# Seven-product weights that begin 256 bytes into their tiles instead of 128

## The chip, the cores and the metric

The kernel runs on one core of a Trainium2 chip. The metric is the device time of one execution in microseconds (us), the median of several runs. TensorE (PE in the rows, with PEld for its weight loads) multiplies, VectorE (DVE) and ScalarE (ACT) prepare operands and evacuate results, GpSimd (POOL) and SyncE (SP) mostly issue DMAs.

## What is computed

One layer of a decoder trunk with sequence 512 and model width 1024, in float32: a combined input projection, gated linear attention (GLA), dilated window attention in three head groups, a gated merge, a squared-ReLU MLP of width 4096, and a sigmoid-gated side input, each behind an RMSNorm. Cut to its products:

```
h   = rmsnorm(x) @ w_in                      # 1024 x 9744, split by columns
mix = (sigmoid(gA) * (oA @ w_o_gla) + sigmoid(gB) * (oB @ w_o_attn)) @ w_out
x  += mix
x  += square(relu(rmsnorm(x) @ w_mlp1)) @ w_mlp2
x  += sigmoid(rmsnorm(x) @ w_pg) * (p @ w_pp)
out = rmsnorm(x)
```

## The kernel before

Every float32 operand is split in two numbers of a reduced format (float32r): `hi`, a rounded copy made by ScalarE, and `lo`, the rest, made by VectorE. A product of two such operands is three matmuls on TensorE: hi with hi, hi with lo, lo with hi.

A weight arrives by DMA as a tile `w` of 128 partitions by 1024 numbers. `fetch` runs a few operands ahead: ScalarE writes the `hi` tile (L244), VectorE the `lo` tile (L239). Both tiles come from `split_weights`. There are 251 such operands, in the fixed order of `OPERANDS`.

Some products are done plainly, with matmuls that stream 512 columns. Others (28 groups, `strassen`) are done in two-by-two blocks with seven block products in place of eight. Their weights are seven operands to a group: four blocks and three sums of blocks. One operand, a stage, is 24 matmuls, each with a 128x128 stationary operand and 256 moving columns, recorded in `run` (L258). In most groups the weight is the stationary operand and an activation (a half of a `ur` tile) moves; in five groups (`v0`, `v1`, `v2`, `gv0`, `gv1`, with `tm=True`) the activation is stationary and the weight moves. In the rows, "mmt<-ur,hi" names the moving operand first and the stationary one second. Side work (attention, GLA, the operand sums) is put between pieces of eight matmuls.

The lines that the change and the argument touch:

```
    def split_weights(tag, i, bufs):
        t = wsp.tile([P, 1024 + PAD], F32R, tag=tag, name=tag, bufs=bufs)
        o = SHIFT if OPERANDS[i] not in UNIT or UNITS[UNIT[OPERANDS[i]]][1] in QUADS else 0
        return t[:, o:o + 1024]
...
                    if tm:
                        c, r = slice(n * P, (n + 1) * P), slice(pr * 256, (pr + 1) * 256)
                        three = ((xh[:, c], wh[:, r]), (xl[:, c], wh[:, r]), (xh[:, c], wl[:, r]))
                    else:
                        c = slice((2 * pr + n) * P, (2 * pr + n + 1) * P)
                        three = ((wh[:, c], xh), (wh[:, c], xl), (wl[:, c], xh))
```

Addresses, in bytes within a partition: a split weight tile is 1152 numbers, 4,608 bytes, nine times 512. The raw weight tiles are 4,096 bytes and the activation tiles 2,048. The three pools stand one behind the other, so all these tiles begin at the same remainder modulo 512. The slices that a matmul takes of them begin at multiples of 512 bytes. So for every seven-product matmul the weight's start and the activation's start differ, modulo 512 bytes, by exactly the shift; for all other products of such tiles, by nothing. "Distance" means this difference below.

The GLA part has 120 matmuls of the same kind, float32r with 256 moving columns (`mm3`, L863), whose operands are all unshifted activation tiles: their distance is nothing.

Of the kernel before, what the change touches and what calls it, by code (L numbers as in the profile page):

```python
# [136 lines left out]

NU, NW, PIECE, WAYS = 71, 5, 8, 2

PAD, SHIFT = 128, 32  # L140

NRAW = 6

# [1418 lines left out]
```

## Time and profile before

| | |
|---|---|
| median of 3 runs | 966.31 us (965.92 to 967.74) |
| the profiled execution | 966.74 us, of which the span from first to last instruction is 964.9 us |
| TensorE busy | 99% of the span, granted clock 0.998 |
| weight loads busy | 93% |
| VectorE, ScalarE, GpSimd busy | 77%, 56%, 11% |

The profiled execution is 0.43 us above the median. Busy time of TensorE counts overlapping matmuls once, and each matmul's record reaches over the start of the next two, so the pace is read from starts: the length of a piece of the chain divided by its matmuls.

### The profile page before, as it was taken

The page shows a single profiled execution, that of the slowest core. Times are in us where ns is not written, and L with a number is a line of the kernel's source. Part 1 is how long each engine was busy: PE and PEld are TensorE (multiplying, and loading weights), DVE is VectorE, ACT ScalarE, POOL GpSimd, SP SyncE. Part 2 cuts the span into 40 slices and gives each one's busy share as a digit, 9 for nine tenths or more (in the row PEclk, how much of TensorE's full clock was granted, in tenths as well). Part 3 has the DMA queues.
Part 4 walks back from the last instruction along what each step waited for, and adds up shares of the span by engine and source line. Part 5 has one row for each costly group of instructions (what it writes and reads, how often), then busy time and mean ns, then how long its engine had stood idle before and what let it go on. Part 6 is the DMA issues. An engine that isn't in the chain of part 4 may idle for free.

```text
span 964.9 us, 16746 instructions
## 1 busy us (share of the span) xinstructions
PE 956.2 (99%) x6732; PEld 893.7 (93%) x6732; DVE 745.4 (77%) x1068; ACT 537.4 (56%) x878; POOL 104.0 (11%) x145
## 2 busy tenths in 40 slices
PE   9999999999999999999999999999999999999997
PEld 7789999999998999999988899999998998988886
DVE  7787879676788769978955788777767899787754
ACT  7346546445666677665732446555655674345633
POOL 0140010420001021013001000010000100000000
PEclk9999999999999999999999999999999999999999
DMA  8565555874446646455536437556654474563102
GB/s 294 159 201 128 153 135 129 236 199 135 110 109 186 164 102 157 113 154 182 169 91 205 119 78 185 153 140 168 170 158 109 113 180 103 132 196 108 44 1 88
DMA packets 41470, 138.93 MB, mean 144 GB/s; under 512 B 5363, under 2 KB 6975, under 8 KB 41392
## 3 DMA queue, kind: packets, MB, share of 16 engines
q1 hardware_dynamic: 27936, 93.29, 29.6%
q0 software_dynamic: 12160, 42.20, 22.1%
q10 hardware_dynamic: 1296, 2.36, 0.7%
q8 instruction: 53, 0.87, 0.4%
q14 instruction: 25, 0.20, 0.1%
HBM read 131.50 MB, written 8.17 MB: 145 GB/s over the span
## 4 chain that ended last, share of the span: by engine, by line
PE 97%; DVE 1%; issue 1%; DMA 1%; ACT 0%; SPq 0%; POOLq 0%; POOL 0%; DVEq 0%; ACTq 0%
PE mmt L258 84%; PE smt L258 4%; PE smt L863 1%; PE smt L803 1%; PE smt L728 1%; DMA u<-in_xT_dram 1%; PE mmt L478 1%; PE mmt L479 0%; PE mmt L477 0%; PE smt L701 0%; PE smt L820 0%; PE smt L819 0%; PE smt L809 0%; PE smt L700 0%; PE smt L991 0%
## 5 line engine op out<-in xcount | busy, mean ns | idle before, releaser
L258 PE MATMUL mmt<-ur,hi 128*128 128x256 f32 (+1 forms) x3152 | 645.3, 302 | 0.0
L258 PEld LDWEIGHTS mmt<-ur,hi 128*128 128x128 f32 x3152 | 506.0, 188 | 24.8 <-issue 1.9
L258 PE MATMUL mmt<-ur,lo 128*128 128x256 f32 (+1 forms) x1576 | 476.9, 303 | 0.0
L239 DVE TENSOR_TENSOR lo<-w,hi 128x1024 fp32r<-128x1024 f32 x251 | 304.2, 1218 | 49.5 <-PE mmt L258 32.1
L244 ACT ACTIVATE hi<-w 128x1024 fp32r<-128x1024 f32 x251 | 262.5, 1054 | 93.2 <-PE mmt L258 28.0
L258 PEld LDWEIGHTS mmt<-ur,lo 128*128 128x128 f32 x1576 | 296.8, 188 | 11.9 <-issue 0.4
L258 PE MATMUL mmt<-hi,ur 128*128 128x256 f32 (+3 forms) x736 | 153.7, 305 | 0.0
L357 ACT ACTIVATE ur<-u 128x512 fp32r<-128x512 f32 x132 | 78.5, 624 | 105.3 <-DVE u L1098 30.9
L258 PEld LDWEIGHTS mmt<-hi,ur 128*128 128x128 f32 x736 | 118.5, 189 | 5.6
L350 DVE TENSOR_TENSOR u<-u,mmt 128x512 f32<-128x512 f32 (+1 forms) x124 | 78.3, 657 | 44.8 <-PE mmt L258 44.6
L258 PE MATMUL mmt<-lo,ur 128*128 128x256 f32 (+3 forms) x368 | 112.2, 305 | 0.0
L365 DVE TENSOR_TENSOR ur<-u,ur 128x512 fp32r<-128x512 f32 x131 | 86.2, 684 | 17.6 <-ACT ur L357 16.9
L332 ACT ACTIVATE u<-mmt 128x512 f32<-128x512 f32 x104 | 61.6, 592 | 55.8 <-PE mmt L258 55.5
L258 PEld LDWEIGHTS mmt<-lo,ur 128*128 128x128 f32 x368 | 69.4, 188 | 2.7
L221 POOL DMA_DIRECT2D w<-in_wts_dram x28 | 24.9, 890 | 356.2 <-DVE w L218 258.3
L210 POOL DMA_DIRECT2D w<-in_wts_dram x28 | 25.8, 921 | 276.5 <-DVE ur L365 52.8
L258 PE MATMUL smt<-ur,hi 128*128 128x512 f32 x144 | 44.7, 390 | 0.1
L224 DVE TENSOR_TENSOR w<-w 128x1024 f32<-128x1024 f32 x28 | 34.3, 1225 | 1.0
L218 DVE TENSOR_TENSOR w<-w 128x1024 f32<-128x1024 f32 x28 | 34.3, 1225 | 1.0
L258 PEld LDWEIGHTS smt<-ur,hi 128*128 128x128 f32 x144 | 26.9, 188 | 6.0 <-DVE ur L365 0.5
L258 PE MATMUL smt<-ur,lo 128*128 128x512 f32 x72 | 28.2, 391 | 0.0
L390 ACT ACTIVATE u<-u 128x512 f32<-128x512 f32 x24 | 14.9, 622 | 16.5 <-DVE u L1179 16.5
(210 smaller groups left out, 715.0 us busy)
## 6 DMA issues: line engine op xcount, KB each, us to landing
w<-in_wts_dram SPq DMA_DIRECT2D x167, 512.0 KB, 4.2
w<-in_wts_dram POOLq DMA_DIRECT2D x56, 512.0 KB, 5.8
u<-in_xT_dram SPq DMA_DIRECT2D x8, 256.0 KB, 5.1
v_dram<-u POOLq DMA_DIRECT2D x8, 256.0 KB, 6.2
u<-v_dram POOLq DMA_DIRECT2D x8, 256.0 KB, 6.6
y_dram<-u ACTq DMA_DIRECT2D x8, 256.0 KB, 2.4
u<-y_dram POOLq DMA_DIRECT2D x8, 256.0 KB, 6.0
u<-in_xT_dram POOLq DMA_DIRECT2D x8, 256.0 KB, 8.6
```

The costliest lines, as they stand in the source:

```text
L210: GP.dma_start(w, wts[UNIT[f"{q}.A22"]], accum_op=OP.add)
L218: V.tensor_tensor(w, w, raw[f"{q}.A11"], op=OP.add)
L221: GP.dma_start(w, wts[UNIT[f"{q}.A21"]], accum_op=OP.add)
L224: V.tensor_tensor(w, w, raw[f"{q}.A12"], op=OP.add)
L239: V.tensor_tensor(lo, w, hi.bitcast(F32), op=OP.subtract)
L244: S.activation(hi, w, AF.Copy)
L258: TE.matmul(o, lhsT=l, rhs=r, start=a, stop=b, skip_group_check=shared)
L332: S.activation(sums[c], bank[b], AF.Copy, scale=-scale if c[0] else scale)
L350: V.tensor_tensor(out, s, ps, op=OP.subtract if m else OP.add)
L357: S.activation(hi, x, AF.Copy)
L365: V.tensor_tensor(lo, x, hi.bitcast(F32), op=OP.subtract)
L390: S.activation(t, x, AF.Square, scale=1.0 / 32.0)
```

## The change

`SHIFT` is counted in numbers of four bytes. The padded tile size stays, and so do all tile addresses. Of the 251 split operands, the 196 of the seven-product groups are written, and read by TensorE, 128 bytes further on in their tiles; the other 55 stay at the start. The instructions on every engine, their order and their waits are the same.

```
-PAD, SHIFT = 128, 32
+PAD, SHIFT = 128, 64
```

## Rows read from the trace of the kernel before

**Rows 1.** The page's first part: busy time, share of the span and instructions of each engine.

```profile
PE 956.2 (99%) x6732; PEld 893.7 (93%) x6732; DVE 745.4 (77%) x1068; ACT 537.4 (56%) x878; POOL 104.0 (11%) x145
```

**Rows 2.** The chain that ended last, by engine; then all that TensorE waited for, by line: total us, times, longest us.

```profile
PE 97%; DVE 1%; issue 1%; DMA 1%; ACT 0%; SPq 0%; POOLq 0%; POOL 0%; DVEq 0%; ACTq 0%
...
PE smt L452 <- POOL ones L447: 1.0, 1, 1.0
PE mmt L478 <- DVE ur L367: 0.3, 1, 0.3
PE mmt L477 <- ACT ur L359: 0.3, 1, 0.3
```

**Rows 3.** TensorE's groups by line and shape: the four kinds of seven-product matmul (256 columns), and the GLA kind of L863. Columns: busy us, mean ns of one, idle time before.

```profile
L258 PE MATMUL mmt<-ur,hi 128*128 128x256 f32 x2576 | 467.0, 283 | 0.0
L258 PE MATMUL mmt<-ur,lo 128*128 128x256 f32 x1288 | 364.4, 283 | 0.0
L258 PE MATMUL mmt<-hi,ur 128*128 128x256 f32 x560 | 101.3, 283 | 0.0
L258 PE MATMUL mmt<-lo,ur 128*128 128x256 f32 x280 | 79.3, 283 | 0.0
L863 PE MATMUL smt<-ur 128*128 128x256 f32 x120 | 16.9, 283 | 0.0
```

**Rows 4.** The chain in order of time, four long pieces made of seven-product matmuls alone: start us, length us, what, count.

```profile
95.85 49.37 PE mmt L258 x416
159.96 14.39 PE mmt L258 x120
608.81 120.57 PE mmt L258 x1016
751.57 40.33 PE mmt L258 x336
```

**Rows 5.** The chain around one of the GLA groups (L863, at distance 0) and the next long seven-product piece: start us, length us, what, count.

```profile
339.94 1.08 PE mmt L258 x9
341.02 1.44 PE smt L863 x12
...
345.79 13.28 PE mmt L258 x112
```

**Rows 6.** Weight loads of L863 and, below, of the commonest kind of L258: count, then duration ns min/median/max, first and last start.

```profile
L863 PEld LDWEIGHTS smt<-ur x120: 187/192/193, 318.3 to 430.4; 128*128 128x128 f32 x120
...
L258 PEld LDWEIGHTS mmt<-ur,hi x3152: 186/188/193, 29.8 to 896.8; 128*128 128x128 f32 x197
```

**Rows 7.** The chain in the attention's scores, matmuls that stream 128 columns: start us, length us, what, count.

```profile
145.22 0.22 PE smt L700 x2
145.44 0.22 PE smt L701 x2
145.66 0.22 PE smt L700 x2
145.88 0.22 PE smt L701 x2
```

**Rows 8.** Windows counted for L258 alone: window, length, TensorE busy and matmuls, granted clock, DMA share, GB/s. The first has plain products alone (512 columns), the second seven-product matmuls of `m2s1c1` and `m2s1c3`.

```profile
490.00:560.00 70.00, 70.00 (x311) 1.00 0.48 143
...
820.00:850.00 30.00, 30.00 (x252) 1.00 0.60 159
```

**Rows 9.** Starts of TensorE's matmuls in a seven-product stretch of the first MLP product: start us, us from the first's start to the last's end, what, count.

```profile
619.80 0.28 PE L258 MATMUL mmt<-ur,lo 128*128 128x256 f32 x1
619.92 0.40 PE L258 MATMUL mmt<-ur,hi 128*128 128x256 f32 x2
...
621.58 0.28 PE L258 MATMUL mmt<-ur,lo 128*128 128x256 f32 x1
```

**Rows 10.** TensorE's groups between 177 and 196 us, where the weight moves and the activation is stationary: busy us, mean ns, idle before.

```profile
L258 PE MATMUL mmt<-hi,ur 128*128 128x256 f32 x108 | 19.4, 281 | 0.0
L258 PE MATMUL mmt<-lo,ur 128*128 128x256 f32 x54 | 15.2, 281 | 0.0
```

**Rows 11.** VectorE's L239 in two windows: length, busy us (count), clock, DMA share, GB/s. In the first the operands are shifted, in the second not.

```profile
610.00:728.00 118.00, 50.07 (x41) 1.00 0.62 161
490.00:560.00 70.00, 15.84 (x13) 1.00 0.48 143
```

**Rows 12.** ScalarE's L244 in the same two windows, same columns.

```profile
610.00:728.00 118.00, 43.48 (x42) 1.00 0.62 161
490.00:560.00 70.00, 13.51 (x13) 1.00 0.48 143
```

## The prediction

> **What bounds the kernel.** I read the page's first part, then the chain and TensorE's waits. TensorE is busy 99% of the span [rows 1], holds 97% of the chain that ended last, and waited for other engines three times, 1.6 us in all, at the very start [rows 2]. So nothing that VectorE, ScalarE or a DMA does decides the end; the time is the number of matmuls times the pace at which TensorE starts them. The change leaves the number and touches what could set the pace: where the operands lie.
>
> Then I read the shapes. Seven-product matmuls are 2576 + 1288 + 560 + 280 = 4704 [rows 3], 24 for each of the 196 shifted operands. All of them are at distance 128 now and go to 256. The reader is to see next what one of them takes from start to start, since 1 ns on each is 4.7 us, 0.49% of the time.
>
> **The pace as it is.** The long pieces of the chain give it [rows 4]. 120.57 us for 1016 is 118.67 ns, and 49.37 us for 416 is 118.68 ns. But 40.33 us for 336 is 120.03 ns, and 14.39 us for 120 is 119.9 ns. So the same shape at the same distance runs in two rhythms: one of 118.7 ns and one of 120.0 ns. The window from 820 to 850 us is another stretch of the slower one: 252 matmuls touch it, two of which began before (a record lasts 283 ns [rows 3], over two steps), so 30 us for 250, 120.0 ns [rows 8]. In the quick rhythm single starts are not even: 15 steps from 619.80 to 621.58 us are again 118.7 ns each, some of them shorter and some longer by a few ns [rows 9].
>
> What sets 120.0? In the window of plain products 311 matmuls touch 70 us, two of them from before it: 70 / 309 = 226.5 ns for 512 columns [rows 8]. At 2.4 GHz, which the granted clock of 1.00 means here, 512 columns stream in 213.3 ns; 13.2 ns are left over. For 256 columns the stream is 106.7 ns, and with the same remainder 119.9 ns. So the slow rhythm is the pace of the stream itself. The load of the next weights hides beneath it: where only 128 columns stream (53 ns), a step takes 0.22 / 2 = 0.11 us [rows 7], and that is the load's pace, about 9 ns under 120. The quick rhythm lies 1.36 ns under the stream's pace.
>
> **Does the distance matter?** One row speaks for it. L863 has the same shape at distance 0, and its group of twelve takes 1.44 us, 120 ns each, while the next long piece at distance 128 takes 13.28 us for 112, 118.6 ns [rows 5]. Its weight loads have a median of 192 ns, where those of L258 have 188 [rows 6]. One row speaks against it: the 336 matmuls and the 120 of [rows 4] run at 120 ns although they are at distance 128, so the rhythm depends at least as much on the state in which a stretch begins. No row shows a distance of 256. The trace therefore bounds the pace after the change, and doesn't give it.
>
> The Trainium skill, "TensorE: Matmul & The Clock Gate", section "Step-by-step: what each phase is for", says that TensorE has two independent read ports in SBUF, and that loading the next weights takes no read bandwidth from the running matmul. By that rule no distance would change anything and the sum would be nothing. The trace agrees in the 120 ns stretches at distance 128, and it is not decided by the 192 against 188 ns of the loads.
>
> **The change part by part.**
>
> Writing the operands 128 bytes further on: nothing. L239 takes 50.07 / 41 = 1.22 us on shifted tiles and 15.84 / 13 = 1.22 us on unshifted ones [rows 11]; L244 takes 43.48 / 42 = 1.04 and 13.51 / 13 = 1.04 us [rows 12]. A move of 128 bytes from the tile's start did nothing to either. Were a copy some per cent longer, it would lie beneath TensorE, which never waits for it [rows 2]; without that cover each 1% of 251 x (1.22 + 1.04) us would be 5.7 us at most.
>
> Instructions, waits, DMAs and tile addresses: nothing is added or moved, and the DMAs write other tiles.
>
> Reading at distance 256, 4704 matmuls. Bound above, from the nearest rows: all go to the rhythm of L863, 120.03 ns. Of the 4704, 120 + 336 [rows 4] and about twice 336 less a little are there already: the second pair of groups in the second MLP product is another 336, of which the window from 820 to 850 us is a part [rows 8]. The sum is 792, and I round it to 800 to 1000 for short stretches. Some 3800 would be slowed by 1.36 ns, 5.2 us. Bound below, also from rows: the pace of the loads, 111 ns, would give 3800 x 7.7 + 900 x 9 = 37 us; but the step from distance 0 to 128 gave only 1.36 of these 9 ns, so a second step of 128 is priced as much again, 5.2 us, an estimate that takes the effect as linear. In between: the rhythms stay as they are, with stretches that change sides. If all that are slow now went to the quick rhythm, this gives 900 x 1.36 = 1.2 us.
>
> I take the value between, nothing. The reason: if distance counts at all, 128 on the one side and 128 on the other give the same pace. Where the weight is stationary it starts 128 bytes after the activation: 118.67 ns [rows 4]. Where it moves, the stationary operand starts 128 bytes before it: from 177 to 196 us 108 + 54 matmuls touch the window, two from before it, 19 us for 160, 118.75 ns [rows 10]. Distance 256 lies between +128 and -128 modulo 512. The sum is 966.74 + 0 for the profiled execution and 966.31 for the median; I say 966.5.
>
> **The rivals.**
>
> *Slower: 256 is like 0.* If what collides repeats every 256 bytes, the change puts the two operands back into step and every seven-product stretch goes to the flat 120.0 ns. For it: L863 at distance 0 is flat at 120 and its loads are longer [rows 5, 6]. Against: the only distances seen modulo 512 can't tell a period of 256 from one of 512, and stretches at distance 128 are at 120 too. Price 5.2 us, 971.9 us. It decides from 1.9 us on, that is when 1400 of the 3800 matmuls in the quick rhythm leave it.
>
> *Faster: 256 is further away than 128.* With a period of 512 bytes and an effect that grows with distance, the pace goes to 118.67 - 1.36 = 117.3 ns. For it: the load alone could go at 111 ns [rows 7], so there is room. Against: the stream's own pace of 120 seems to have nothing to do with distance, and the quick rhythm is only 1% under it. Price -5.2 us, 961.5 us.
>
> *No effect whatever,* by the ports: the same time as the forecast, with the rhythms where they are.
>
> *More than these:* a new rhythm in which steps last as long as the load's record grew at L863, 4 ns, on all 4704: 19 us, 985 us. Nothing in the trace shows a steady pace like it.
>
> **How the numbers follow.** A measurement of this kernel can tell about 0.2%, 1.9 us, from no change. The chances: forecast and no effect together 0.43; slower to 971.9 us 0.31; faster to 961.5 us 0.17; more than these 0.05 above and 0.04 below. So faster by over 0.2% 0.21, within 0.2% 0.43, slower by over 0.2% 0.36. The likeliest is 966.5 us, its own range 965 to 968. Since cases of both signs hold over half of the chance, the range for 8 in 10 takes in both rivals: 961 to 972.5 us.
>
> **What would show it.** The two long pieces of 1016 and 416 matmuls are the test: at 120.6 and 49.4 us again, the distance of 256 is as good as 128. At 121.9 and 49.9 us they are flat at 120 ns, and the slower rival holds; at 119.2 and 48.8 us, the faster. L863's twelve should stay at 1.44 us, and L239 and L244 at 1.22 and 1.04 us, as should the plain products at 226.5 ns. The forecast is wrong if the pieces move by more than 0.4 ns a matmul, and the reading of a TensorE that waits for nobody is wrong if the pieces stay and the time doesn't.

## The result and the profile after

The changed kernel takes 970.36 us (median of 5, 970.29 to 970.76) against 965.92 us for the kernel before: 1.0045 times as long, interval 1.0033 to 1.0056. That is 4.4 us slower, well clear of 0.2%, inside the range of 961 to 972.5 us, and it is not the case that the prediction held likeliest: it is the slower rival, whose price was 971.9 us. (One execution of a later kernel, the changed one with a gap, took 5390.54 us where its other three took 972.82 to 974.19; its time and its trace stand behind no number here.)

The pieces of the chain that were named as the test, after the change (start us, length us, what, count):

```profile
95.02 49.91 PE mmt L258 x416
159.74 14.39 PE mmt L258 x120
611.04 121.92 PE mmt L258 x1016
755.17 40.31 PE mmt L258 x336
```

Beside [rows 4]: the 1016 matmuls went from 120.57 to 121.92 us, 118.67 to 120.0 ns each; the 416 from 49.37 to 49.91 us. The two pieces that were at 120 ns before are where they were (14.39, and 40.31 for 40.33 us). The quick rhythm is gone from the two pieces that had it.

The weight loads of the commonest seven-product kind and of L863 after (count, then duration ns min/median/max, first and last start):

```profile
L258 PEld LDWEIGHTS mmt<-ur,hi x3152: 186/192/193, 29.0 to 900.3; 128*128 128x128 f32 x197
...
L863 PEld LDWEIGHTS smt<-ur x120: 187/192/192, 318.8 to 431.9; 128*128 128x128 f32 x120
```

The median for L258 was 188 ns in [rows 6], and is now the 192 of L863, the kind at distance 0. By its pace and by its loads, distance 256 behaves as distance 0.

What was expected not to move did not. TensorE's waits after (total us, times, longest us) are still three sources, 1.8 us at the very start:

```profile
PE smt L452 <- POOL ones L447: 1.0, 1, 1.0
PE mmt L478 <- DVE ur L367: 0.5, 2, 0.3
PE mmt L477 <- ACT ur L359: 0.3, 1, 0.3
```

The twelve of L863 (start us, length us) and the window of plain products (length, TensorE busy and matmuls, clock, DMA share, GB/s) are as before, 120 ns a matmul and 311 in 70 us:

```profile
341.72 1.44 PE smt L863 x12
...
490.00:560.00 70.00, 70.00 (x311) 1.00 0.49 143
```

VectorE's L239 and ScalarE's L244 in the page's costliest groups (busy us, mean ns, idle before): 1.219 and 1.053 us on average, at the new place in the tile as at the old.

```profile
L239 DVE TENSOR_TENSOR lo<-w,hi 128x1024 fp32r<-128x1024 f32 x251 | 304.4, 1219 | 51.5 <-PE mmt L258 35.8
L244 ACT ACTIVATE hi<-w 128x1024 fp32r<-128x1024 f32 x251 | 262.3, 1053 | 92.1 <-PE mmt L258 28.6
```

### The profile page after: what moved, and what is told of

Same layout as the page of the kernel before. It is cut to its first block, busy times and chain, and to the rows that moved or that the text cites. A ratio compares the mean times of both kernels' runs of the same rounds, so it can differ in the third digit from the quotient of the medians.

```text
span 968.4 us, 16746 instructions
## 1 busy us (share of the span) xinstructions
PE 959.6 (99%) x6732; PEld 897.6 (93%) x6732; DVE 746.0 (77%) x1068; ACT 537.5 (56%) x878; POOL 103.8 (11%) x145
## 3 DMA queue, kind: packets, MB, share of 16 engines
q10 hardware_dynamic: 1296, 2.36, 0.6%
## 4 chain that ended last, share of the span: by engine, by line
PE 97%; DVE 1%; issue 1%; DMA 0%; ACT 0%; SPq 0%; POOLq 0%; POOL 0%; DVEq 0%; ACTq 0%
PE mmt L258 84%; PE smt L258 4%; PE smt L863 1%; PE smt L803 1%; PE smt L728 1%; PE mmt L478 1%; PE mmt L479 0%; PE mmt L477 0%; DMA u<-in_xT_dram 0%; PE smt L819 0%; PE smt L809 0%; PE smt L701 0%; PE smt L700 0%; PE smt L820 0%; PE smt L1397 0%
## 5 line engine op out<-in xcount | busy, mean ns | idle before, releaser
L258 PE MATMUL mmt<-ur,hi 128*128 128x256 f32 (+1 forms) x3152 | 648.9, 303 | 0.0
L258 PEld LDWEIGHTS mmt<-ur,hi 128*128 128x128 f32 x3152 | 509.8, 190 | 24.8 <-issue 1.9
L258 PE MATMUL mmt<-ur,lo 128*128 128x256 f32 (+1 forms) x1576 | 477.8, 303 | 0.0
L239 DVE TENSOR_TENSOR lo<-w,hi 128x1024 fp32r<-128x1024 f32 x251 | 304.4, 1219 | 51.5 <-PE mmt L258 35.8
L244 ACT ACTIVATE hi<-w 128x1024 fp32r<-128x1024 f32 x251 | 262.3, 1053 | 92.1 <-PE mmt L258 28.6
L258 PEld LDWEIGHTS mmt<-ur,lo 128*128 128x128 f32 x1576 | 299.9, 190 | 11.9 <-issue 0.4
L258 PE MATMUL mmt<-hi,ur 128*128 128x256 f32 (+3 forms) x736 | 154.5, 306 | 0.0
L258 PEld LDWEIGHTS mmt<-hi,ur 128*128 128x128 f32 x736 | 119.7, 191 | 5.5
L258 PE MATMUL mmt<-lo,ur 128*128 128x256 f32 (+3 forms) x368 | 112.4, 306 | 0.0
L258 PEld LDWEIGHTS mmt<-lo,ur 128*128 128x128 f32 x368 | 70.2, 191 | 2.7
L258 PE MATMUL smt<-ur,hi 128*128 128x512 f32 x144 | 44.7, 391 | 0.1
L258 PEld LDWEIGHTS smt<-ur,hi 128*128 128x128 f32 x144 | 26.9, 188 | 6.0 <-DVE ur L365 0.5
L258 PE MATMUL smt<-ur,lo 128*128 128x512 f32 x72 | 28.1, 391 | 0.0
```

Source lines behind the costliest of these rows:

```text
L239: V.tensor_tensor(lo, w, hi.bitcast(F32), op=OP.subtract)
L244: S.activation(hi, w, AF.Copy)
L258: TE.matmul(o, lhsT=l, rhs=r, start=a, stop=b, skip_group_check=shared)
```

## The experiments

The theory after the result: what counts is the distance between the starts of TensorE's two operands, the moving one and the weights that it loads, and its effect repeats every 256 bytes (P256). The rivals: that the further the weights lie into their tiles the worse (U), that the place in the tile counts and not the distance (absolute), and, later, that the state in which a stretch begins decides its rhythm (entry).

**Six other distances.** Each is one number in one line:

```
-PAD, SHIFT = 128, 32
+PAD, SHIFT = 128, 0      # and 96, 16, 48, 8, 24
```

Distance 0 (no shift):

> All split weights begin at the start of their tiles, distance 0. Theory P256 (what collides repeats every 256 bytes, so 0 and 256 are the same): flat 120.0 ns a seven-product matmul, the piece of 1016 takes 121.9 us, loads have a median of 192 ns, and the time is that of the changed kernel, 970 to 971 us. Rival U (256 is bad for another reason, for instance any distance over 128): distance 0 keeps some other pace; if 0 is harmless the time stays near 966 us.

Distance 384:

> Distance 384 bytes. Theory P256: 384 is 128 modulo 256, so the quick rhythm of 118.7 ns returns: the piece of 1016 takes 120.6 us, loads 188 ns, 966 us. Rival U (the further the worse): flat 120 ns or slower, 970.4 us or more. Rival linear with a period of 512: 384 is 128 from the other side, also 966 us, but then 256 should have been better than 128, which it was not.

Distance 64:

> Distance 64 bytes. Theory P256 with a penalty near step only: 64 is as good as 128, 966 us and 118.7 ns. If the effect grows linearly from 0 to 128: half of the 1.3 ns, 119.3 ns, 968 us. If the period were 128 with some other cause, 64 would be the best of all, below 965 us.

Distance 192:

> Distance 192 bytes, the mirror of 64 modulo 256. Theory P256, symmetric: the same as distance 64. Where the sign counts (the load follows the stream or runs ahead of it), 64 and 192 differ, and each of the two kernels has the other's distance in its five groups with moving weights. Rival U (the further the worse): between 966 and 970.4 us.

Distance 32:

> Distance 32 bytes. At 64 bytes there were two rhythms, 113.3 and 117.8 ns, against 118.7 and 120.0 at 128 and 120.0 alone at 0 and 256. Theory near-step (what hurts is that load and stream begin in the same place, and a period of 256 or less): 32 lies between 0 and 64, so a time between 953 and 970 us. Rival odd multiples (only multiples of 128 bytes hurt): 32 is as good as 64, 953 us, or better if more stretches take the rhythm of 113.3 ns (940 us if all did).

Distance 96:

> Distance 96 bytes, between 64 (953 us) and 128 (966 us). Theory near-step: between these two, about 958 us. Rival odd multiples: as good as 64, 953 us, with a different share of stretches at 113.3 ns, since which of the two rhythms a stretch takes seemed to hang on how it is entered.

What was measured. The paces are the lengths of the pieces of 1016 and of 336 matmuls, divided by their counts; in both pieces the weights are stationary:

| distance, bytes | time, us | ratio to before, interval | 1016, ns each | 336, ns each |
|---|---|---|---|---|
| 0 | 970.34 | 1.0047 (1.0035 to 1.006) | 120.0 | 120.0 |
| 32 | 961.86 | 0.9957 (0.9943 to 0.9971) | 118.3 | 118.3 |
| 64 | 953.19 | 0.9865 (0.985 to 0.9881) | 113.3 | 117.8 |
| 96 | 962.41 | 0.9963 (0.995 to 0.9975) | 117.4 | 117.3 |
| 128 (before) | 965.92 | 1 | 118.7 | 120.0 |
| 192 | 958.5 | 0.9922 (0.9909 to 0.9936) | 117.8 | 117.8 |
| 256 (the change) | 970.36 | 1.0045 (1.0033 to 1.0056) | 120.0 | 120.0 |
| 384 | 965.99 | 1.0002 (0.9993 to 1.0011) | 118.7 | 120.0 |

Distance 0, the two pieces in the chain (start us, length us, what, count):

```profile
611.17 121.92 PE mmt L258 x1016
755.27 40.31 PE mmt L258 x336
```

Distance 384:

```profile
607.68 120.57 PE mmt L258 x1016
750.48 40.33 PE mmt L258 x336
```

Distance 64:

```profile
602.68 115.15 PE mmt L258 x1016
740.02 39.58 PE mmt L258 x336
```

Distance 192:

```profile
603.00 119.66 PE mmt L258 x1016
744.85 39.57 PE mmt L258 x336
```

Distance 0 repeats the changed kernel to a hundredth of a microsecond in both pieces, and 384 repeats the kernel before. So 0 and 256 are the same, and so are 128 and 384: at these distances the effect repeats every 256 bytes, and U is out (384 is furthest of all and as good as 128). What no theory had priced is how much there was to win: 64 bytes make the kernel 12.7 us faster than 128. A period of 128, the one theory with 64 as the best of all, is out, since 128 is 4.4 us faster than 0. A gain that grows evenly from 0 to 128 is out too: in time, 32 and 96 lie between 64 and its neighbours, and 128 is slower than all three. 192, the mirror of 64, has the same rhythms of 113.3 and 117.8 ns, but in other stretches. That only multiples of 128 bytes hurt is also out, since 32 and 96 are about 9 us slower than 64.

At 32 and 96 bytes the table hides a difference. In two pieces of 112 matmuls, the weight moves in nearly all of the first (so the stationary operand begins 32 or 96 bytes before the moving one) and is stationary in the second. Distance 32, these two and then the pieces of the table:

```profile
343.33 13.08 PE mmt L258 x112
427.83 13.25 PE mmt L258 x112
605.57 120.23 PE mmt L258 x1016
747.98 39.76 PE mmt L258 x336
```

Distance 96:

```profile
345.34 13.42 PE mmt L258 x112
430.11 13.14 PE mmt L258 x112
607.73 119.23 PE mmt L258 x1016
749.13 39.42 PE mmt L258 x336
```

Where the weight moves, the steps are 116.8 and 119.8 ns at 32 and 96; where it is stationary, 118.3 and 117.3. So the sign may count at these distances. No run here separates it from the way in which a stretch is entered, which comes below.

**Distance or place?** A pool of 128 bytes was put between the split weights and the activations, which moves every activation tile on by 128 bytes:

```
+    gap = ctx.enter_context(tc.tile_pool(name="gap", bufs=1))
+    gap.tile([P, 32], F32, name="gap")
     ar = ctx.enter_context(tc.tile_pool(name="ar", bufs=NU))
```

With the weights of the kernel before, 128 bytes into their tiles, so that the distance becomes 0:

> The kernel before (weights 128 bytes into their tiles) with the same gap of 128 bytes ahead of the activations: distance 0 for the seven-product operands though the weights' shift is untouched. Theory relative: flat 120.0 ns, loads of 192 ns, 970.4 us, slower by 0.45% without any change of SHIFT. Rival absolute: 966 us.

Measured: 976.58 us, ratio 1.0111 (1.0097 to 1.0125). The chain (L260 is the former L258):

```profile
96.14 49.91 PE mmt L260 x416
614.68 121.91 PE mmt L260 x1016
736.59 22.31 PE smt L260 x96
758.90 40.30 PE mmt L260 x336
```

The seven-product pieces are at 120.0 ns though their weights lie where they lay before. The total was expected at 970.4 us and is 6 us above it, and the third row says where: 96 plain matmuls of 512 columns, now at distance 128, take 22.31 us, 232.4 ns each. In the changed kernel, where they are at distance 0, the same piece is

```profile
795.48 21.79 PE smt L258 x96
```

227.0 ns each. The expectation had put nothing on the plain products, and they are not indifferent: 5.4 ns on 1296 of them is 7 us.

With the weights of the changed kernel, 256 bytes in, so that the distance becomes 128:

> The changed kernel (weights 256 bytes into their tiles), but all activation tiles begin 128 bytes later, behind a gap: the distance of seven-product operands is 128 again, and the plain products, whose weights stay at the start of their tiles, go from 0 to 128 too. Theory relative (what counts is the distance between the two operands of TensorE): the quick rhythm of 118.7 ns is back, 966 us, as if nothing had been changed. Rival absolute (what counts is where in its tile or in SBUF the weight begins, for instance for the copies that write it): it stays at 120.0 ns and 970.4 us. Plain products: 226.5 ns unless the distance moves them.

Measured: 973.51 us, the median of three executions, ratio 1.0077 (1.0062 to 1.0093): above both values expected, as the plain products cost time here too. A second measurement of the same kernel, with a trace:

> The same kernel as the one with 256 bytes and a gap of 128, for a readable trace. With the gap of 128 bytes alone the plain products, at distance 128 there, took 232.4 ns instead of 227.1: 1296 of them, 6.8 us. Theory relative: seven-product matmuls at 118.7 ns, the piece of 1016 at 120.6 us, so 966 + 6.8 = 972.7 us. Rival absolute: 120.0 ns, the piece at 121.9 us, 977 us as with the shift of 128 and the gap.

Measured: 972.28 us, ratio 1.0063 (1.0043 to 1.0084), as expected by the relative theory with the plain products' 6.8 us. But its chain:

```profile
96.54 49.37 PE mmt L260 x416
612.09 121.92 PE mmt L260 x1016
756.38 39.86 PE mmt L260 x336
```

The quick rhythm is back in the 416 (118.7 ns) and is new in the 336 (118.6 ns, 120.0 in both kernels), though the weights lie where the changed kernel has them, and with the weights of the kernel before it was gone. So the place in the tile doesn't set the rhythm, and absolute is out. The 1016, expected at 120.6 us, are at 120.0 ns each: at distance 128 both rhythms exist, and here the 1016 and the 336 changed sides. The distance sets which rhythms there are, and something else picks one.

**What picks the rhythm?** At 64 bytes the stretches of 336, which begin right behind plain products, were at 117.8 ns, and the 1016 at 113.3. With 64 bytes, the first matmul of three groups was done as two of 128 columns (a split):

```
+    if kick and not mms and op == "A11":
+        mms.append((o[:, 0:P], l, r[:, 0:P], True, False))
+        mms.append((o[:, P:HT], l, r[:, P:HT], False, False))
+        continue
```

> Distance 64 bytes, and the first matmul of three groups that follow plain products (the first of the first MLP product, and one for each column half of the second) is done as two matmuls of 128 columns. At 64 bytes the long stretches that followed plain products took the rhythm of 117.8 ns, others 113.3. Theory entry (the rhythm is chosen by how a stretch is entered and is then kept): the two stretches of 336 go to 113.3 ns, 40.3 us less 1.5 each, together 3 us less than the 953.2 us at 64 bytes, minus 0.3 us for the three more matmuls. Rival place (these stretches are slow because of their operands): 953.5 us, no change of rhythm.

Measured: 952.42 us, ratio 0.9862 (0.9847 to 0.9876). My split for the second MLP product stood at the first chunk of each column half; these two groups follow one another, so one split fell inside the first stretch of 336 and the second stretch, of the third chunk, had none. That makes it a control:

```profile
603.16 116.06 PE mmt L258 x1024
...
741.41 38.50 PE mmt L258 x338
...
801.69 84.49 PE mmt L258 x534
```

The first stretch, 338 matmuls with its two splits, fell from 39.58 to 38.50 us. The piece of 534, which holds the unsplit one (336, and 198 plain), is the 84.49 us that it is at 64 bytes without splits. The split at the start of the first MLP product moved nothing: 1024 matmuls, 113.3 ns each as without it. The median was 0.8 us under 953.19 us and not the 2.7 us expected, with ranges that overlap (952.35 to 953.89 against 952.73 to 953.63); the expectation had counted both stretches, and only one had a split. What this run shows stands in the pieces, not in the total.

Moving and stationary weights at different shifts, so that the stationary operand always begins 64 bytes after the moving one, modulo 256:

```
+        q = OPERANDS[i].rpartition(".")[0] + ".A11"
+        o = 0 if q not in UNIT else 3 * SHIFT if UNITS[UNIT[q]][1] == "quadt" else SHIFT
```

> Weights 64 bytes into their tiles where they are stationary, 192 bytes where they move, so that the stationary operand begins 64 bytes after the moving one, modulo 256, in all seven-product matmuls. Theory sign (the load is better off ahead): the 840 matmuls with moving weights go from 117.6 to between 113.3 and 116, 1.3 to 3.5 us less than 953.2 us. Rival entry (only the entry decides, both signs allow both rhythms): the five groups may go either way, and the time is within 2 us of 953.2 us.

Measured: 951.75 us, ratio 0.9849 (0.9833 to 0.9866), 1.4 us under the 953.19 of one shift for all. A stretch of moving weights, 120 matmuls, at 64 bytes for all and, below, here (two kernels' chains):

```profile
159.17 14.13 PE mmt L258 x120
```

```profile
157.98 13.62 PE mmt L259 x120
```

117.7 and 113.5 ns. With 192 bytes for all, where its operands lie as here, it takes as long:

```profile
158.61 13.62 PE mmt L258 x120
```

So far that fits the sign. But the stretch of 336, with stationary weights, is at 117.8 ns with 64 bytes and with 192, so neither sign secures the quicker rhythm; the gain in time alone doesn't decide between the theories. The next run has a piece that does.

**Both, with the splits in place.** Splits at the start of the first MLP product, at the first and third chunk of the second, and inside the piece of 416, at the group of q2:

> The kernel with 64 bytes for stationary and 192 bytes for moving weights, and four first matmuls done as two of 128 columns: at the start of the first MLP product, at the first and third chunk of the second MLP product in its first column half (each follows plain products), and at the group of q2, in the middle of a stretch in the rhythm of 117.8 ns. Theory entry: both stretches of 336 go to 113.3 ns (the one of the third chunk stayed at 117.8 before, without a split of its own), 1.5 us each, and the first of the first MLP product 0.4 us; the four extra matmuls cost about 0.25 us together: 951.75 - 3.4 + 0.3 = 948.6 us. If a split inside a stretch changes the rhythm too, the 336 matmuls behind it in the piece of 416 give 1.5 us more, 947 us. Rival place: nothing moves, 952 us.

Measured: 948.21 us (947.6 to 949.34), ratio 0.9818 (0.9804 to 0.9831). The chain (L259 is the former L258):

```profile
95.07 47.64 PE mmt L259 x417
...
158.16 14.13 PE mmt L259 x120
172.56 20.16 PE mmt L259 x176
...
737.27 38.36 PE mmt L259 x337
...
797.41 83.13 PE mmt L259 x535
```

The kernel with the two shifts and no splits has these:

```profile
94.40 48.98 PE mmt L259 x416
171.77 21.87 PE mmt L259 x184
738.15 39.58 PE mmt L259 x336
799.51 84.49 PE mmt L259 x534
```

The three pieces with a split lose 1.2 to 1.4 us with one matmul more in each. Of 336 matmuls at 4.4 ns 1.5 us were expected, less the split's own 0.06. The operands, their addresses and their order are the same, so a disturbance at a stretch's entry, or inside it, can switch its rhythm and the operands don't fix it. The splits also moved stretches that have none: the 120 with moving weights went back from 13.62 to 14.13 us, 117.8 ns, with its operands where they were, so the sign of the distance doesn't secure the quicker rhythm there either; the stretch behind it went the other way, from 118.9 to 114.5 ns. What in an entry decides is therefore open, and the gain is that of these splits in this order of work. The expectation had 947 us for the case in which a split inside a stretch works; the split of the first MLP product again gave nothing, and the 120 lost 0.5 us. This kernel beats both: 17.7 us under the kernel before and 22 under the changed one. Its range lies wholly below that of the two shifts alone (950.93 to 952.05 us), so the gain isn't that of one execution. By then VectorE's `lo` (L240) has 1.5% of the chain; whether it is the next limit wasn't tried.

What wasn't tried: distances that aren't multiples of 32 bytes, 32 and 96 with either sign for all groups, a distance other than 0 and 128 for the plain products, and a disturbance at every entry.

## Why the prediction was wrong in its likeliest case

The measured 970.36 us lies within 961 to 972.5 us because the range took in both rivals. The likeliest value, 966.5, was missed: the measurement lies outside its own range of 965 to 968.

*TensorE sets the time and waits for nobody; writing the operands elsewhere costs nothing.* Right, by the rows of after above.

*1 ns on each of 4704 matmuls is 4.7 us; the pieces of 1016 and 416 are the test.* Right. They moved by 1.3 ns and the kernel by 4.4 us.

*"I take the value between, nothing", because 256 lies between +128 and -128 modulo 512.* This is the step that failed. It assumed a period of 512 bytes. The measurement at 384 and at 0 shows 256 to be no middle but the same place as 0. The rows of before could not tell 256 from 512, as the rival said; the argument from the two sides holds only under the longer period, and I counted it as if it spoke for that period.

*The slower rival: everything flat at 120 ns, 5.2 us.* Its mechanism is what happened; it had a chance of 0.31, behind the 0.43 that rested on the step above. Its size was a little large: 4.4 us measured. The step of 1.36 ns was 1.33 (118.67 to 120.0), and the short pieces rose by less: the chain's seventeen pieces of eight take 0.94 to 0.96 us before and after. L863, the one row at the distance in question if the period is 256, foretold the pace and the loads' 192 ns to the nanosecond.

*The faster rival, by an effect that grows with distance.* Wrong in its form: 256 is worse than 128. But that there was room under 118.7 ns, which it drew from the loads' 111 ns, was right, and the room was nearer, at 64 bytes: 113.3 ns.

*"So the slow rhythm is the pace of the stream itself."* Wrong, and it was held against the faster rival. The same 256 columns went at 113.3 ns at 64 bytes, 6.6 ns over the prediction's 106.7 and not 13.2, so 120.0 is not what the stream must take.

*The 120 ns stretches at distance 128 speak against an effect of distance.* A misreading. 120.0 ns occurs at distance 128 as one of two rhythms, and at 0 and 256 as the only one seen in long stretches. That one distance has two rhythms does not say that distance is without effect.

*By the skill's rule no distance would change anything.* "TensorE: Matmul & The Clock Gate", section "Step-by-step: what each phase is for", of the Trainium skill has two independent read ports, and a load of the next weights that takes no read bandwidth from the running matmul. The trace doesn't agree with what the prediction drew from that: with the same instructions the kernel takes 970.3 us at distance 0 and 953.2 us at distance 64, and TensorE's waits, 1.0 and 2.0 us in the two traces, don't account for it. Whether the load takes bandwidth from the stream or something else slows the pair, no run here shows.

## What to carry to other kernels

Where TensorE never waits and streams 256 columns for each weight load, look at the starts, not the busy time, and at where the two operands lie to one another: here 64 bytes were worth 1.8% against none. Scan such an offset finely before settling on one (0, 128 and 256 are all poor here, and 64 is not), and try stationary and moving weights apart: at 32 and 96 bytes their paces differed. When stretches of identical matmuls run in two paces, look at how each is entered, and at what a disturbance there does to the stretches behind it.

## What the runs showed of the hardware

TensorE's pace depends on the distance, within a partition, between the starts of its moving operand and of the weights that it loads. For 256 columns of float32r the steady step was 120.0 ns at 0 and 256 bytes, 118.7 or 120.0 at 128 and 384, and 113.3 or 117.8 at 64 and 192; the pieces shown at 32 and 96 lie from 116.8 to 119.8. With 512 columns, in the plain products, distance 0 (227.0 ns) was better than 128 (232.4 ns), the other way round than with 256; that the width is the reason is not shown. It is shown that the pair of addresses counts and not one of them alone, since moving the weights or moving the activations gave and took the effect, and that one distance has two steady rhythms, between which a disturbance can switch. How the two addresses slow one another, and what in an entry picks the rhythm, stays open.
